# Layer 1 of a float32 decoder trunk: the first two SwiGLU pairs by seven products, and the sums of x on another engine

## The chip, the cores and the metric

One Trainium2 chip; the kernel runs on one of its cores. The core has a matrix engine (TensorE: PE for its matmuls, PEld for its weight loads, which overlap them), VectorE (DVE), ScalarE (ACT), GpSimd (POOL) and SyncE (SP, which issues most of the transfers from memory). Each of them takes its instructions in the order in which the program holds them, and waits at an instruction until the semaphores that it names have reached their values. The metric is the time of one execution on the device in microseconds (us), and the kernel before and the changed one are compared by it.

## What is computed

Two decoder layers over 512 tokens of 1024 channels, in float32. Layer 0 is a Conformer convolution block and a SwiGLU feed-forward; layer 1 is a sliding-window attention and a second SwiGLU feed-forward; a final RMSNorm ends it. The change lies in the feed-forward of layer 1, whose reference is this:

```python
def rmsnorm(x, g):
    xf = x.astype(jnp.float32)
    xf = xf * lax.rsqrt(jnp.mean(xf * xf, axis=-1, keepdims=True) + EPS)
    return (xf * g.astype(jnp.float32)).astype(x.dtype)

def swiglu_ffn(x, w_up, w_down):
    gate, up = jnp.split(x @ w_up, 2, axis=-1)
    return (jax.nn.silu(gate) * up) @ w_down
...
        h = h + swiglu_ffn(rmsnorm(h, norm_ffn[l]), ffn_w_up[l], ffn_w_down[l])
```

The hidden width is 2816, so `w_up` is 1024 x 5632 and `w_down` 2816 x 1024.

## The kernel before

**Float32 by three matmuls.** A float32 operand is held as two reduced-precision parts, hi and lo. `mm3` (its three matmuls are lines 380, 381 and 382) adds hi x hi, hi x lo and lo x hi. Weights come in chunks of 128 x 1024 floats (512 KB): SP loads a chunk into one of six `raw` tiles (line 261), ACT copies it to `whi` (line 294), and DVE subtracts to get `wlo` (line 297). Loads run up to nine chunks ahead of their use, the two splits three chunks ahead; `advance` does both. `PLAN` lists the chunks in the order in which TensorE takes them.

**Pairs.** The 22 slices of 128 hidden columns are worked off as 11 pairs. A plain pair (`plain_pair`) takes four chunks, `up` of half 0 and 1 of the channels for gate and up: 96 matmuls of 512 tokens. A pair by seven products (`SevenPair`, `seven_pair`) is a Winograd form of Strassen's scheme: the weight block and x are cut into 2 x 2 blocks (for x: `B11`, `B12`, `B21`, `B22`, channels by tokens), and seven products of sums of blocks take the place of eight. Each product is one chunk and 24 matmuls of 256 tokens, 168 for the pair. The products are named by their weight blocks: A11, A12, A22 are plain blocks, S1 to S4 are sums of blocks; their partners are B11, B21, T4, and T1, T2, T3 and B22 (`SEVEN`). So A11, A12 and S4 need no sum of x, and S1, S2, S3 and A22 do. `take` runs one product and moves its result out of PSUM into the four quarters of the pair's tile `up`; S2, S3, S4 and so on add into shared accumulation chains in PSUM (`CHAINS`): x for A11, S2, S3 and A22, z for S1 and S4, y for A12.

**Sums of weights.** S1 to S4 of every pair are made in memory by DMA while the kernel runs: SP copies one block (line 275), and a DMA issued by POOL adds the other onto it (line 289). `prepare` is the list of these, `share` says how many of them go with one chunk.

**Sums of x.** `Rows.sums` has ACT scale the eight slices of h into float32 tiles (line 753), then makes T1, T2, T3 and T4 one after the other (line 759, on POOL), each followed by its split into hi (ACT, lines 541 and 544) and lo (DVE, lines 542 and 545).

**The start of layer 1's feed-forward.** The output projection of the attention is added to h by DVE (line 1547); for each of the eight slices of h, ACT makes the hi part of the scaled x (line 536) and the square of h (line 487), DVE makes the lo part (line 537) and adds the square to the running sum (line 491). `Rms.step1` then has TensorE sum that over the channels with four short matmuls (line 503); DVE adds the epsilon (line 505), POOL takes the power -1/2 (line 507), DVE puts it on a diagonal (line 510). `step2` spreads it with one matmul (line 529), and the gates use it (lines 793 and 849).

The loop over `STEPS1` is: pair 0 plain, with the sums of x made beside it; pair 1 by seven products, with `flip` after each product (four transposes of h on TensorE, line 1562, and a copy by ACT, line 1563); pair 2 by seven; then the lower product `low` of pairs 0 and 1 (line 902), and so on to pair 10.

**What sets the order.** The program is written once in Python; a scheduler then places each engine's instructions by priorities and its own guess of when each is ready. So the order of the rows on each engine is part of the program, and is shown below where the change moves it.

Of the kernel before, what the change touches and what calls it, by code (L numbers as in the profile page):

```python
# [18 lines left out]
P = 128  # L19
# [4 lines left out]
FT = FF // P  # L24
# [13 lines left out]
STEPS1 = [("up", 0), ("up", 1), ("up", 2), ("low", 0)]  # L38
# [19 lines left out]
SEVENS = tuple(range(1, FT // 2))  # L58

def by_seven(layer, pair):  # L60
    return pair in SEVENS if layer else pair >= HALVES0[1][0]


def ups(layer, pair):
    return [("up", layer, pair, half, which) for half in range(2) for which in range(2)]
# [26 lines left out]
def chunk_plan():  # L92
# [12 lines left out]
    for part in range(2):  # L105
        pw2()
        for pair in range(*HALVES0[0]):
            plan.extend(ups(0, pair))
        downs(*HALVES0[0])
        if part == 0:  # L110
            plan.extend(("up0", pair, "A12") for pair in FIRST)
# [12 lines left out]
    for kind, pair in STEPS1:  # L124
        plan.extend(blocks_of(kind, pair) if kind == "low" or by_seven(1, pair) else ups(1, pair))
# [84 lines left out]
def hybrid_trunk(ctx: ExitStack, tc: tile.TileContext, xT, W, prm_in, wdw_in, sinks, relb, onehot, fin, lead, out):  # L210
# [524 lines left out]
    class Rows:  # L735
# [13 lines left out]
        def sums(self):  # L749
# [7 lines left out]
            for name, t, f, a, b in (("T1", t1, nc.gpsimd.tensor_sub, b11, b12), ("T2", b11, nc.gpsimd.tensor_add, b22, t1),  # L757
                                     ("T3", b12, nc.gpsimd.tensor_sub, b22, b12), ("T4", b21, nc.gpsimd.tensor_sub, b11, b21)):
                pool_op(f(t, a, b))
# [3 lines left out]
                split([both[:, e] for e in range(2)], t, name == "T2")  # L763

    def new_gates(pool):
        return pool.tile([P, 2, 2, 2, 256], F32, tag="up", name=uid("up"), bufs=3)

    def plain_pair(pair, rows, pool):

        banks = accs(512)  # L770
        steps = None
        for half in range(2):
            for which in range(2):
                w = get("up", 1, pair, half, which)
                order = [(k, m) for k in range(4) for m in range(2)]
                if half == 1:
                    order = [(k, m) for m in range(2) for k in range(4)]
                for k, m in order:
                    mm3(banks[which * 2 + m], [a[:, k, m * P:(m + 1) * P] for a in w], rows.x[half * 4 + k],
                        half == 0 and k == 0, half == 1 and k == 3)  # L780
                if half == 0 and which == 0:
                    rows.rms.step1()
                    continue

                if pair == 0:
                    steps = steps or rows.sums()
                    for _ in range(1 + half):
                        next(steps, None)
        rs_bc = rows.rms.step2().rearrange("p (s q) -> p s q", s=2)
        c = new_gates(pool)  # L790
        for m in range(2):
            t = temp()
            nc.vector.tensor_mul(t.rearrange("p (s q) -> p s q", s=2), banks[m].rearrange("p (s q) -> p s q", s=2), rs_bc)
            nc.scalar.activation(t, t, AF.Silu)
            nc.vector.tensor_mul(c[:, m, :, 0, :], banks[2 + m].rearrange("p (s q) -> p s q", s=2),
                                 t.rearrange("p (s q) -> p s q", s=2))
        return c
# [14 lines left out]
    class SevenPair:  # L812

        def __init__(self, kind, pair, rows, c, c11=None):
            self.kind, self.pair, self.rows, self.c, self.early = kind, pair, rows, c, c11
            self.chains = {}

        def take(self, a):
            c11, c12, c21, c22 = (self.c[:, m, s] for m in range(2) for s in range(2))
            chain = CHAINS[a][0]  # L820
# [10 lines left out]
            elif a == "S1":  # L831
                nc.scalar.mul(c22, r, -1.0)
            elif a == "S2":
# [517 lines left out]
    if True:  # L1351
# [10 lines left out]
        share[0] = 1  # L1362
# [204 lines left out]
    for kind, pair in STEPS1:  # L1567
# [6 lines left out]
        if by_seven(1, pair):  # L1574
# [3 lines left out]
        if pair == SEVENS[0]:  # L1578
            flip()
# [118 lines left out]
```

## Time and profile before

| | |
|---|---|
| runs | 1043.85 us median of 3 (1043.27 to 1044.0) |
| the profiled execution | 1043.27 us, of which the span from the first to the last instruction is 1041.5 us |
| mean granted TensorE clock | 0.997 |
| attention, to the end of the output projection | about 560 to 697 us of the span |
| pair 0 of layer 1 (plain) | about 697 to 720 us |
| pairs 1 and 2, with the first lower product | about 720 to 787 us |
| then every two pairs with a lower product | 59.7 us |

Times in the profile are microseconds from the start of the span. A row of the timeline gives start, duration, engine, line, operation, output<-input, partitions, shape and type, the number of instructions merged into the row, and in brackets how long the engine was idle before and what ended it. A matmul's recorded duration overlaps that of the next; the distance from start to start is what one costs in a row of them.

### The profile page before, as it was taken

To read this page: it belongs to the slowest core of one execution; us is meant where nothing else is said; L and a number is where in the kernel's file an instruction comes from. 1 tells how busy PE (TensorE), PEld (TensorE's weight loads), DVE (VectorE), ACT (ScalarE), POOL (GpSimd) and SP (SyncE) were. 2 spreads that over 40 slices of the span, in tenths; PEclk is the share of its full clock that TensorE was granted. 3 is DMA by queue.
4 is the path that set the end of the run, shared out by engine and by line. 5 is a ranking of instruction groups with operands and counts; after the bars stand their busy time and mean duration, and the time that the engine had idled before them with its cause. 6 is when DMAs were issued, how large, how long until landed. Compare 5 with 4: busy or idle time off the path is not lost.

```text
span 1041.5 us, 17709 instructions
## 1 busy us (share of the span) xinstructions
PE 1031.5 (99%) x6580; PEld 932.6 (90%) x6580; DVE 776.5 (75%) x1202; ACT 613.0 (59%) x1062; POOL 473.2 (45%) x569
## 2 busy tenths in 40 slices
PE   9999999999999999999999999999999999999996
PEld 8888889999988999998888877788989999898995
DVE  3999989978789777673536566678686877868777
ACT  3887798847776556552333565466655556554654
POOL 3999999930535233221214255405442334434134
PEclk9999999999999999999999999999999999999998
DMA  9999747999999988999969766955879988877742
GB/s 356 340 315 207 205 126 204 272 256 275 249 239 262 304 220 284 256 301 244 286 209 254 210 183 183 228 154 152 252 230 312 287 264 264 245 233 222 224 150 81
DMA packets 67282, 248.33 MB, mean 238 GB/s; under 512 B 7579, under 2 KB 13884, under 8 KB 66364
## 3 DMA queue, kind: packets, MB, share of 16 engines
q1 hardware_dynamic: 54236, 200.75, 55.9%
q0 software_dynamic: 12672, 46.14, 24.8%
q8 instruction: 51, 0.84, 0.3%
q10 hardware_dynamic: 288, 0.31, 0.1%
q14 instruction: 35, 0.29, 0.1%
HBM read 241.93 MB, written 97.52 MB: 326 GB/s over the span
## 4 chain that ended last, share of the span: by engine, by line
PE 98%; DMA 0%; DVE 0%; issue 0%; POOLq 0%; SPq 0%; POOL 0%; ACT 0%
PE bank L380 20%; PE bank L382 20%; PE bank L381 20%; PE bank L960 10%; PE bank L902 9%; PE bank L412 4%; PE bank L378 4%; PE bank L413 2%; PE bank L1441 1%; PE bank L1483 1%; PE bank L1470 1%; PE bank L1058 1%; PE bank L1607 1%; PE bank L948 1%; DMA both<-in_lead_dram 0%; PE bank L1562 0%
## 5 line engine op out<-in xcount | busy, mean ns | idle before, releaser
L297 DVE TENSOR_TENSOR wlo<-raw,whi 128x1024 fp32r<-128x1024 f32 x246 | 329.7, 1348 | 136.8 <-ACT whi L294 136.5
L294 ACT CAST whi<-raw 128x1024 fp32r<-128x1024 f32 x246 | 257.1, 1049 | 276.6 <-PE bank L381 194.1
L380 PE MATMUL bank<-quad,whi 128*128 128x256 f32 (+1 forms) x976 | 307.4, 317 | 0.0
L381 PE MATMUL bank<-quad,whi 128*128 128x256 f32 (+1 forms) x976 | 306.6, 315 | 0.0
L382 PE MATMUL bank<-quad,wlo 128*128 128x256 f32 (+1 forms) x976 | 305.7, 315 | 0.0
L380 PEld LDWEIGHTS bank<-quad,whi 128*128 128x128 f32 x976 | 185.5, 191 | 12.8 <-issue 1.6
L381 PEld LDWEIGHTS bank<-quad,whi 128*128 128x128 f32 x976 | 186.0, 191 | 11.9 <-issue 0.5
L382 PEld LDWEIGHTS bank<-quad,wlo 128*128 128x128 f32 x976 | 185.6, 191 | 11.8 <-issue 0.4
L853 POOL TENSOR_TENSOR up<-up 128x512 f32<-128x512 f32 x34 | 62.9, 1851 | 283.6 <-ACT up L850 283.6
L1002 POOL TENSOR_TENSOR pr<-pr,pr 128x256 f32<-128x256 f32 x208 | 155.4, 788 | 2.6 <-ACT pr L1001 2.5
L380 PE MATMUL bank<-rows,whi 128*128 128x256 f32 x488 | 138.0, 283 | 0.0
L381 PE MATMUL bank<-rows,whi 128*128 128x256 f32 x488 | 137.8, 282 | 0.0
L382 PE MATMUL bank<-rows,wlo 128*128 128x256 f32 x488 | 137.8, 282 | 0.0
L1009 DVE SCALAR_TENSOR_TENSOR bank<-apad,wdw,bank 128x256 f32<-128x256 f32 x248 | 112.4, 485 | 3.4
L1001 ACT ACTIVATE pr<-apad,wdw 128x256 f32<-128x256 f32 x208 | 98.3, 502 | 14.9 <-POOL pr L1002 13.1
L960 PE MATMUL bank<-quad,w 128*128 128x256 f32 x448 | 98.7, 380 | 0.0
L960 PEld LDWEIGHTS bank<-quad,w 128*128 128x128 f32 x448 | 84.9, 190 | 11.8 <-DVE bank L1009 0.2
L380 PEld LDWEIGHTS bank<-rows,whi 128*128 128x128 f32 x488 | 93.1, 191 | 0.3
L381 PEld LDWEIGHTS bank<-rows,whi 128*128 128x128 f32 x488 | 93.1, 191 | 0.3
L382 PEld LDWEIGHTS bank<-rows,wlo 128*128 128x128 f32 x488 | 93.0, 191 | 0.0
L491 POOL TENSOR_TENSOR tmp<-tmp,tmp 128x256 f32<-128x256 f32 (+1 forms) x28 | 26.8, 957 | 101.4 <-ACT tmp L487 96.2
L412 PE MATMUL bank<-quad,whi 128*128 128x512 f32 x168 | 59.7, 398 | 0.0
(230 smaller groups left out, 1635.9 us busy)
## 6 DMA issues: line engine op xcount, KB each, us to landing
raw<-in_W_dram SPq DMA_DIRECT2D x170, 512.0 KB, 5.7
raw<-sum SPq DMA_DIRECT2D x88, 512.0 KB, 5.4
sum<-in_W_dram SPq DMA_DIRECT2D x52, 512.0 KB, 6.2
sum<-in_W_dram POOLq DMA_DIRECT2D x44, 512.0 KB, 9.6
sum<-sum POOLq DMA_DIRECT2D x44, 512.0 KB, 8.5
sum<-in_W_dram SPq DMA_DIRECT2D x4, 3584.0 KB, 30.4
w<-in_W_dram SPq DMA_DIRECT2D x14, 512.0 KB, 8.6
sum<-in_W_dram SPq DMA_DIRECT2D x4, 1024.0 KB, 30.3
```

Of the source, the lines that this page charges most:

```text
L294: on_act = nc.scalar.copy(hi, src).ins
L297: latest[:] = [on_act, lo_engine[0].tensor_sub(lo, src, f32(hi)).ins]
L380: nc.tensor.matmul(out, w[0], x[0], start=start, stop=False, **kw)
L381: nc.tensor.matmul(out, w[0], x[1], start=False, stop=False, **kw)
L382: nc.tensor.matmul(out, w[1], x[0], start=False, stop=stop, **kw)
L412: nc.tensor.matmul(first[2], first[0], first[1], start=start, stop=False)
L853: pool_op(nc.gpsimd.tensor_mul(gate, gate, c[:, m, :, 1, :]))
L902: nc.tensor.matmul(out, x, w[:, ws], start=first and e == 0 and i == 0, stop=e == 1 and i == 2, skip_group_check=True)
L960: mm = nc.tensor.matmul(self.pb[:, w * W2:(w + 1) * W2], w1_of(ct, w, k), x[k] if x else xg[k][:, tok], start=k == 0, stop=k == KT - 1)
L1001: on_act = nc.scalar.mul(pr, a[:, j:j + W2], tap(j))
L1002: on_pool = pool_op(nc.gpsimd.tensor_add(pr, acc, pr))
L1009: on_dve = nc.vector.scalar_tensor_tensor(yt if i == nd - 1 else c, src, tap(i), c if i else self.shift, op0=ALU.mult, op1=ALU.add)
```

## The change

Pairs 0 and 1 are both done by seven products, as one step `("two", 0)`, in the order of the list `TWO`: A11 of both pairs, A12 of both, S4 of both (the six that need no sum of x), then S1, S2, S3, A22 of pair 0, and the same of pair 1. Since S4 now comes ahead of S1, S4 gets an accumulation chain of its own, "w" (`apart`), and its result is added on DVE to what S1 and S2 give. `step1` is called after the first product, and the eight flips after products 7 to 14. The sums of x, T1 to T4, are made by DVE in place of POOL, one step of them with most products and two with products 3 to 6. `share` is 1.2 in place of 1 from the key and value projection to the end of attention, since four more sums of weights are due. `plain_pair` goes.

```diff
-STEPS1 = [("up", 0), ("up", 1), ("up", 2), ("low", 0)]
+STEPS1 = [("two", 0), ("up", 2), ("low", 0)]
+TWO = [(p, a) for a in ("A11", "A12", "S4") for p in range(2)] + [(p, a) for p in range(2) for a in ("S1", "S2", "S3", "A22")]
...
-        plan.extend(blocks_of(kind, pair) if kind == "low" or by_seven(1, pair) else ups(1, pair))
+        plan.extend([("up", *step) for step in TWO] if kind == "two" else blocks_of(kind, pair))
...
-            for name, t, f, a, b in (("T1", t1, nc.gpsimd.tensor_sub, b11, b12), ("T2", b11, nc.gpsimd.tensor_add, b22, t1),
-                                     ("T3", b12, nc.gpsimd.tensor_sub, b22, b12), ("T4", b21, nc.gpsimd.tensor_sub, b11, b21)):
-                pool_op(f(t, a, b))
+            yield
+            for name, t, f, a, b in (("T1", t1, nc.vector.tensor_sub, b11, b12), ("T2", b11, nc.vector.tensor_add, b22, t1),
+                                     ("T3", b12, nc.vector.tensor_sub, b22, b12), ("T4", b21, nc.vector.tensor_sub, b11, b21)):
+                with tc.issue_after(latest[1]):
+                    f(t, a, b)
                 yield
...
                 split([both[:, e] for e in range(2)], t, name == "T2")
+                yield
...
-    def plain_pair(pair, rows, pool):
...
-        def __init__(self, kind, pair, rows, c, c11=None):
+        def __init__(self, kind, pair, rows, c, c11=None, apart=False):
...
-            chain = CHAINS[a][0]
+            chain = "w" if self.apart and a == "S4" else CHAINS[a][0]
...
             elif a == "S1":
                 nc.scalar.mul(c22, r, -1.0)
+                if self.apart:
+                    nc.vector.tensor_add(c12, r, c12)
+            elif self.apart and a in ("S2", "S4"):
+                (nc.scalar.copy if a == "S4" else lambda o, i: nc.vector.tensor_add(o, i, c12))(c12, r)
...
-        share[0] = 1
+        share[0] = 1.2
...
-        if by_seven(1, pair):
-            c = seven_pair("up", pair, nxt, new_gates(pool7), flip if pair == SEVENS[0] else None)
-        else:
-            c = plain_pair(pair, nxt, pool7)
-        if pair == SEVENS[0]:
-            flip()
+        if kind == "two":
+            two = [SevenPair("up", p, nxt, new_gates(pool7), apart=True) for p in range(2)]
+            steps = nxt.sums()
+            for n, (p, a) in enumerate(TWO):
+                two[p].take(a)
+                if n == 0:
+                    nxt.rms.step1()
+                for _ in range((1, 2)[n in (2, 3, 4, 5)]):
+                    next(steps, None)
+                if n >= 6:
+                    flip()
+                if a == "A22":
+                    forms[p] = forms_of(two[p].gates(), pool7, p % 2)
+            continue
+        c = seven_pair("up", pair, nxt, new_gates(pool7))
```

In the changed program most lines stand a little higher: `mm3` is lines 376 to 378, `step1`'s matmuls are line 499, the split of weights lines 290 (ACT) and 293 (DVE), the sums of x line 757.

TensorE, where `step1` stands. Before, in pair 0: `quad_7167` and `quad_7168` are hi and lo of the second half of x's channels, `quad_7165` and `quad_7166` those of the first, and `tmp_7353` is the finished sum of squares.

```order
L381 MATMUL bank_7356<-quad_7168,whi_7362 128x512
L382 MATMUL bank_7356<-quad_7167,wlo_7363 128x512
L381 MATMUL bank_7357<-quad_7168,whi_7362 128x512
L503 MATMUL bank_7390<-ones_c,tmp_7353 128x1 x4
L380 MATMUL bank_7358<-quad_7165,whi_7304 128x512
L381 MATMUL bank_7358<-quad_7166,whi_7304 128x512
```

In the changed program, at the end of the first product (A11 of pair 0, into `bank_7370`) and the start of the second (A11 of pair 1, into `bank_7424`); `tmp_7365` is the finished sum of squares:

```order
L377 MATMUL bank_7370<-quad_7175,whi_7283 128x256
L378 MATMUL bank_7370<-quad_7174,wlo_7284 128x256
L499 MATMUL bank_7402<-ones_c,tmp_7365 128x1 x4
L376 MATMUL bank_7424<-quad_7174,whi_7316 128x256
L377 MATMUL bank_7424<-quad_7175,whi_7316 128x256
L378 MATMUL bank_7424<-quad_7174,wlo_7317 128x256
```

Before, 47 matmuls of 512 tokens of pair 0 stand ahead of the four matmuls of `step1`; now 24 matmuls of 256 tokens do. Up to the first matmul of pair 0 TensorE's order is the same in both programs, and so is that of DVE and ACT up to the last addition of squares.

VectorE from that last addition (`tmp_7353` before) on. Before, `wlo` are weight splits, `rows` the lo parts of sums of x, `ms` and the product with `ident` belong to the norm:

```order
L491 TENSOR_TENSOR tmp_7353<-tmp_7347,tmp_7353 128x512
L297 TENSOR_TENSOR wlo_7449<-raw_7176,whi_7448 128x1024
L545 TENSOR_TENSOR rows_7476<-t_7441,rows_7476 128x1024
L505 TENSOR_SCALAR ms_7395<-bank_7390 128x4
L542 TENSOR_SCALAR rows_7480<-quad_7431,rows_7480 128x1024
L545 TENSOR_TENSOR rows_7514<-quad_7431,rows_7514 128x1024
L297 TENSOR_TENSOR wlo_7487<-raw_7209,whi_7486 128x1024
L510 TENSOR_TENSOR tmp_7399<-ident,rs_7397 128x512
```

In the changed program (`wlo_7464` is the split for S4 of pair 0, `wlo_7500` for S4 of pair 1, `wlo_7536` for S1 of pair 0; line 757 makes T1, T2, T3):

```order
L487 TENSOR_TENSOR tmp_7365<-tmp_7359,tmp_7365 128x512
L757 TENSOR_TENSOR t_7423<-quad_7413 128x1024
L501 TENSOR_SCALAR ms_7407<-bank_7402 128x4
L506 TENSOR_TENSOR tmp_7411<-ident,rs_7409 128x512
L1543 TENSOR_SCALAR nrs<-rs_7409 128x4
L293 TENSOR_TENSOR wlo_7464<-raw_7185,whi_7463 128x1024
L757 TENSOR_TENSOR quad_7413<-quad_7414,t_7423 128x4x256
L541 TENSOR_TENSOR rows_7492<-t_7423,rows_7492 128x1024
L538 TENSOR_SCALAR rows_7528<-quad_7413,rows_7528 128x1024
L293 TENSOR_TENSOR wlo_7500<-raw_7221,whi_7499 128x1024
L757 TENSOR_TENSOR quad_7413<-quad_7414,quad_7413 128x4x256
L808 TENSOR_TENSOR up_7368<-bank_7457,up_7368 128x512
```

The norm's instructions now stand ahead of the split for S4 of pair 0, and the four sums of x and their lo parts share DVE's queue with the splits.

More of the change, by code (lines that the diff above doesn't have):

```diff
@@ L57, with ups @@
 SEVEN = ("A11 B11", "S1 T1", "S2 T2", "A12 B21", "S3 T3", "S4 B22", "A22 T4")
[L58 to L65, printed above, removed]
+def ups(pair):
+    return [("up", 0, pair, half, which) for half in range(2) for which in range(2)]
 SUMS = {"S1": ("A21", "A22"), "S2": ("A11", "S1"), "S3": ("A21", "A11"), "S4": ("A12", "S2")}
@@ L107, in chunk_plan @@
         for pair in range(*HALVES0[0]):
-            plan.extend(ups(0, pair))
+            plan.extend(ups(pair))
         downs(*HALVES0[0])
```

29 lines of the change are left out of this document (1 added, 28 removed).

## The prediction

> **What bounds the kernel now.** I read the page first: who is busy, and the chain of work that ended last.
>
> ```profile
> PE 1031.5 (99%) x6580; PEld 932.6 (90%) x6580; DVE 776.5 (75%) x1202; ACT 613.0 (59%) x1062; POOL 473.2 (45%) x569
> PE 98%; DMA 0%; DVE 0%; issue 0%; POOLq 0%; SPq 0%; POOL 0%; ACT 0%
> ```
>
> TensorE is the chain. The view of its waits, next, names two, both in the first 8 us:
>
> ```profile
> PE bank L465 <- POOL ones_m L462: 1.1, 1, 1.1
> PE bank L948 <- DVE quad L922: 0.7, 2, 0.4
> ```
>
> So time is won only by fewer or shorter matmuls, and lost by any new wait of TensorE. The question is what both are at the start of layer 1's feed-forward. TensorE's timeline there, and three rows of the chain further on:
>
> ```profile
> 696.75 0.39 PE L380 MATMUL bank<-quad,whi 128*128 128x512 f32 x1
> ...
> 707.18 0.39 PE L381 MATMUL bank<-quad,whi 128*128 128x512 f32 x1
> 707.41 0.95 PE L503 MATMUL bank<-ones_c,tmp 128*128 128x1 f32 x8
> 708.21 0.49 PE L380 MATMUL bank<-quad,whi 128*128 128x512 f32 x1
> ```
>
> ```profile
> 821.03 5.52 PE bank L902 x24
> 829.42 11.09 PE bank L902 x48
> 880.73 5.52 PE bank L902 x24
> ```
>
> Pair 0 begins at 696.75; 47 matmuls stand ahead of step1 at 707.41, so one of 512 tokens costs 10.66 / 47 = 0.227 us. From 821.03 to 880.73 lie two pairs by seven (336 matmuls of 256) and one lower product (84 of line 902, at 11.09 / 48 = 0.231, 19.4 us): one of 256 tokens costs (59.70 - 19.4) / 336 = 0.120 us.
>
> **TensorE's work.** Pair 0 loses 96 x 0.227 = 21.8 us and gets 168 x 0.120 = 20.1 us: **1.6 us less**. The eight flips, the four matmuls of step1 and the spread of the norm move but stay as many. This is all that the change can give, since TensorE waits for nothing that it removes.
>
> **The new wait.** step1 now stands behind 24 matmuls of 256. TensorE takes them in order, so it comes to step1 at 696.75 + 24 x 0.120 = 699.63. What step1 reads is the last sum of squares, and DVE makes it here:
>
> ```profile
> 697.57 0.68 DVE L1547 TENSOR_TENSOR h<-bank,h 128x512 f32<-128x512 f32 x1
> 698.17 0.68 DVE L491 TENSOR_TENSOR tmp<-tmp,tmp 128x512 f32<-128x512 f32 x1
> 698.77 1.22 DVE L297 TENSOR_TENSOR wlo<-raw,whi 128x1024 fp32r<-128x1024 f32 x1
> 699.90 0.74 DVE L537 SCALAR_TENSOR_TENSOR quad<-h,prm,quad 128x512 fp32r<-128x512 f32 x1
> 700.57 0.68 DVE L491 TENSOR_TENSOR tmp<-tmp,tmp 128x512 f32<-128x512 f32 x1
> 701.17 0.74 DVE L537 SCALAR_TENSOR_TENSOR quad<-h,prm,quad 128x512 fp32r<-128x512 f32 x1
> 701.83 0.68 DVE L491 TENSOR_TENSOR tmp<-tmp,tmp 128x512 f32<-128x512 f32 x1
> ```
>
> Without a pause from 697.57 on, it ends at 701.83 + 0.68 = 702.51, and up to there the three engines' orders are unchanged, so it ends there in the changed kernel too. Before, TensorE came to step1 4.9 us after it; now it comes 2.88 us ahead. How fast a waiting TensorE starts shows at the very start of the trace:
>
> ```profile
> 3.96 0.35 DVE L922 TENSOR_SCALAR quad<-both,prm 128x256 f32<-128x256 f32 x1 [3.09 <-DMA prm<-in_prm_dram]
> 4.36 0.29 PEld L948 LDWEIGHTS bank<-quad,both 128*128 128x128 f32 x1 [0.68 <-DVE quad L922]
> ...
> 706.95 0.19 PEld L381 LDWEIGHTS bank<-quad,whi 128*128 128x128 f32 x1
> ```
>
> DVE ended at 4.31, the weight load began at 4.36: 0.05 us. The load itself takes 0.19 us and can't go ahead here, since its operand is what is waited for. So step1 begins at 702.51 + 0.05 + 0.19 = 702.75 in place of 699.63: **3.1 us lost**. Bounds: 2.9 (neither of the two small terms) to 3.4 (the first matmul behind it as slow as behind step1 above, 0.33 from 708.21 on against 0.23, and a slower semaphore). Behind step1 in TensorE's queue stand A11 of pair 1 and all the rest, and A11 of pair 1 was ready: its splits come well ahead.
>
> **What is late next.** step1 takes 0.8 us (707.41 to 708.21), so product 2 begins at 703.55, and each product takes 24 x 0.120 = 2.88. I follow DVE's new order from 702.5. It holds 128x1024 operations, for which these rows of DVE, POOL and ACT give prices:
>
> ```profile
> 705.96 8.07 DVE L297 TENSOR_TENSOR wlo<-raw,whi 128x1024 fp32r<-128x1024 f32 x1 [3.44 <-ACT whi L294]
> 716.29 1.22 DVE L545 TENSOR_TENSOR rows<-quad,rows 128x1024 fp32r<-128x1024 f32 x1
> 724.96 1.65 DVE L297 TENSOR_TENSOR wlo<-raw,whi 128x1024 fp32r<-128x1024 f32 x1 [0.25 <-ACT whi L294]
> 707.93 5.01 POOL L759 TENSOR_TENSOR quad<-quad,quad 128x1024 f32<-128x1024 f32 x2
> 715.32 1.96 POOL L507 TENSOR_TENSOR rs<-ms,mhalf 128x4 f32<-128x4 f32 x1 [2.38 <-DVE ms L505]
> 699.96 5.02 ACT L753 ACTIVATE quad<-h,prm 128x512 f32<-128x512 f32 x8
> 704.88 1.04 ACT L294 CAST whi<-raw 128x1024 fp32r<-128x1024 f32 x1
> ```
>
> A sum of x on DVE isn't in the trace. Below stands 1.2 us, a subtraction of the same shape beside an idle POOL; above 1.65, beside a working one. (The 8.07 us is a DVE operation that stood until POOL's sums of x were done; with those gone from POOL that goes too, but TensorE didn't wait for it.) I take 1.2, since POOL has no large operation there now. T1 from 702.5 to 703.7; then the norm, which waits for step1 and for POOL's 1.96 us, so its DVE part ends at about 706.6; the split for S4 of pair 0 ends at 707.8. Product 5 (S4 of pair 0) begins at 703.55 + 3 x 2.88 = 712.2: 4.4 us to spare. Up to the split for S1 of pair 0 DVE has six more of 1.2 and one of 0.7, to about 715.7; product 7 begins at 718.0: 2.3 us to spare. Its ACT part is no later: the scaling of x ends at 705.0, and ACT then needs about 1.05 us for each of three splits, the first two sums' hi parts and two copies, to 712.6. Behind product 7 each further product brings a 1.2 us split and a 0.7 us addition to DVE against 2.88 us and the flips on TensorE, so the distance grows. The sums thus cost nothing under this cover of 2.3 us; it is there because step1 waits. Without the wait of step1 it would be about gone.
>
> **Transfers.** Three more chunks are loaded, four more copies and four more additions issued, half of them far ahead of use. The extra additions fall in the attention:
>
> ```profile
> L289 POOL DMA_DIRECT2D sum<-in_W_dram x7 | 5.9, 979 | 0.0
> L1460 POOL TENSOR_SCALAR sc<-sc,sm 128x256 f32<-128x256 f32 (+1 forms) x64 | 31.4, 505 | 44.0 <-DVE sm L1458 43.7
> ```
>
> ```profile
> 697.00:707.00 10.00, 10.00 (x46) 8.29 (x45) 6.56 (x9) 9.87 (x15) 4.34 (x3) 1.00 0.36 117
> 821.00:880.70 59.70, 59.70 (x422) 56.11 (x421) 45.24 (x50) 32.53 (x42) 21.51 (x19) 1.00 0.88 275
> ```
>
> An addition takes POOL 0.98 us to issue; four take 4 us of the 44 in which POOL, by its groups from 575 to 690 us, waits for DVE there. Behind them are the softmax's scalings, which TensorE's transposes read; their cost is 0 under that cover, and up to 1 us each if one meets a scaling. The opening of pair 0 uses the DMA engines 0.36 of the time against 0.88 in the steady part (the last two rows, of the windows; the share is the last number but one), which feeds pairs by seven at the same pace. I take 0.
>
> **Sum.** -1.6 + 3.1 + 0 = **+1.5 us**. Against the profiled execution, 1043.27 us (a span of 1041.5 and 1.8 around it), that is 1044.8; the median before is 0.58 above that execution, so the forecast for the median is **1045.4 us**, +0.15%. A change within 0.2%, 2.1 us, can hardly be told from none here.
>
> **Rivals.**
>
> *The clock drops in the wait.* TensorE has no long pause before, but it has one at the end. Its last matmul in the timeline, the windows there (the granted clock is the last number but two), and a row of the timeline and one of the chain on the price:
>
> ```profile
> 1033.05 0.28 PE L1607 MATMUL bank<-whi,hid 128*128 128x256 f32 x1
> ```
>
> ```profile
> 1032.80:1036.20 3.40, 0.53 (x5) 0.32 (x3) 3.18 (x9) 2.55 (x8) 1.65 (x3) 1.00 0.62 231
> 1036.20:1036.30 0.10, 0.00 (x0) 0.00 (x0) 0.10 (x1) 0.00 (x0) 0.10 (x1) 0.70 0.00 0
> ```
>
> ```profile
> 1.05 2.93 PE L465 MATMUL bank<-ones_m 128*128 128x128 f32 x12 [1.05 <-POOL ones_m L462]
> ...
> 593.13 1.46 PE bank L1470 x12
> ```
>
> The last matmul ended at 1033.33, and the clock fell between 1036.20 and 1036.30, 2.9 us later; the new pause is 2.7 to 2.9 us. At half clock a matmul costs twice: 12 took 2.93 us at the cold start against 1.46 later. That start lasted at least these 2.93 us; an episode of 3 to 6 us would lose 1.5 to 3 us more. Time 1045.4 + 1.5 to 3, say **1047.6**. [...] Chance 0.18.
>
> *DVE becomes the bound.* If its fifteen 128x1024 operations between the sum of squares and S1 of pair 1 take 1.65 us in place of 1.2, that is 6.7 us against a cover of 2.3: 4.4 us more, 1049.8; with half of that inflation 1 us, 1046.4. Against it: POOL has only its short power and issues there. Say **1047.5**, chance 0.16.
>
> *No wait.* If the squares are done when TensorE comes, all of the 1.6 us is won: **1042.2**. It needs DVE 2.9 us earlier, and DVE has no pause to give. Chance 0.10.
>
> *The change doesn't do what it says* (the pairs run, but a transfer of a weight sum is late): for S4 of pair 0, the first sum used, a landing late by one median of POOL's additions, 9.1 us, less the 4.4 us spare, gives 1050. Chance 0.04.
>
> **How the numbers follow.** The forecast has 0.50, its own range 1044.6 to 1046.4 from the bounds of the wait and the 0.7 us between the runs before; the cases above 0.18, 0.16, 0.10 and 0.04, and 0.02 for the unforeseen. Slower by over 0.2% is above 1045.94: a quarter of the forecast's range (0.13), nearly all of clock, DVE and late transfer (0.35): 0.48. Faster is below 1041.76: the case without a wait ends just inside, so 0.06 for it with luck. The rest, 0.46, is within. The range from 1042.1 to 1047.9 holds the forecast, the case without a wait and the lower halves of the others.
>
> **What would show it.** Right: an idle time of TensorE of about 3 us ahead of step1's line, released by DVE's addition of squares, and no other over 0.3 us up to the first lower product; DVE's 8 us row gone; the same granted clock. Wrong: no pause there; a granted clock under 1 in a window from 703 to 710; pauses ahead of S1 to A22 of pair 0 that end with a `rows` or `wlo` of DVE; a scaling in the attention that ends a pause of TensorE.

## The result, and the profile after

| | before | changed |
|---|---|---|
| median of six runs each | 1043.92 us (1043.27 to 1044.3) | 1048.55 us (1047.03 to 1049.71) |
| ratio of the changed kernel's times to those before, 95% interval | | 1.0046, 1.0033 to 1.0059 |
| the profiled execution (span) | 1043.27 us (1041.5) | 1047.03 us (1045.3) |
| mean granted clock, run by run | 0.997 (profiled) | 0.997, 0.996, 0.996, 0.995, 0.994, 0.996 |

The changed kernel is slower: by 4.6 us between the medians, by 0.46% in the ratio. The forecast was 1045.4 and its range ended at 1047.9, so the time lies outside it, on the slow side.

The page first: who is busy, and the shares of the chain that ended last.

```profile
PE 1032.0 (99%) x6652; PEld 936.1 (90%) x6652; DVE 781.4 (75%) x1212; ACT 618.3 (59%) x1069; POOL 468.0 (45%) x571
PE 97%; DVE 1%; issue 1%; DMA 0%; ACT 0%; POOLq 0%; POOL 0%; DVEq 0%
```

At this level the two kernels look alike: PE has lost one point of the chain, and DVE and "issue" have one each. The view of TensorE's waits says what is new:

```profile
PE bank L499 <- DVE tmp L487: 2.8, 1, 2.8
PE bank L378 <- DVE wlo L293: 0.9, 1, 0.9
```

(Total us, times, the longest.) Neither was there before. The first is the wait that was forecast, at step1. The second was not forecast. TensorE's timeline shows both, and a third thing that no view of waits can show:

```profile
696.18 0.28 PE L376 MATMUL bank<-quad,whi 128*128 128x256 f32 x1
...
698.93 0.28 PE L378 MATMUL bank<-quad,wlo 128*128 128x256 f32 x1
702.00 1.05 PE L499 MATMUL bank<-ones_c,tmp 128*128 128x1 f32 x8 [2.79 <-DVE tmp L487]
...
704.47 0.42 PE L376 MATMUL bank<-quad,whi 128*128 128x256 f32 x1
...
707.85 0.28 PE L377 MATMUL bank<-quad,whi 128*128 128x256 f32 x1
...
784.37 0.39 PE L378 MATMUL bank<-quad,wlo 128*128 128x256 f32 x1 [0.94 <-DVE wlo L293]
...
824.57 0.63 PE L874 MATMUL bank<-whi,fhi 128*128 128x512 f32 x2
```

From 698.93 to 702.00 are 3.07 us where a matmul takes 0.12: **2.95 us of wait**. (The rows count two records for each plain float32 matmul: x8 are the four of step1.) Behind it the matmuls run at 0.12 us each for a while, and then, from 704.47 to 707.85, 16 of them take 0.21. The windows between the borders of that stretch (PE's busy time and count come second, the granted clock is the last number but two):

```profile
697.54:700.95 3.41, 1.67 (x14) 1.47 (x13) 3.41 (x6) 3.41 (x7) 0.00 (x0) 1.00 0.21 19
700.95:704.36 3.41, 2.36 (x20) 2.36 (x21) 2.29 (x4) 3.41 (x7) 0.93 (x1) 1.00 0.70 288
704.36:707.77 3.41, 3.41 (x18) 3.41 (x18) 3.17 (x5) 2.41 (x4) 1.85 (x3) 0.50 0.52 84
707.77:711.18 3.41, 3.41 (x30) 3.41 (x30) 3.36 (x3) 3.35 (x4) 0.00 (x0) 1.00 1.06 222
```

The granted clock is 0.50 for 3.41 us and 1.00 on both sides. It falls 2.4 us after TensorE has taken up work again, which is why the pause and the slow matmuls don't touch in the timeline. Cost: 3.38 us for 16 matmuls that take 1.92 at full clock, **1.46 us**. TensorE is "busy" all the while, so neither the busy shares nor the waits show it.

DVE's new work at the start of the feed-forward runs as the sum had it: T1 takes 1.23 us, the splits about it the same, and there is no row of 8 us.

```profile
702.05 1.23 DVE L757 TENSOR_TENSOR t<-quad 128x1024 f32<-128x1024 f32 x1
```

The second new wait lies 80 us later, in the first lower product. The rows of DVE and POOL that lead to it in the changed kernel, and below them those of the same place before (lines 297 and 909 there):

```profile
780.00 4.32 DVE L293 TENSOR_TENSOR wlo<-raw,whi 128x1024 fp32r<-128x1024 f32 x1
...
780.41 2.81 POOL L881 TENSOR_TENSOR h<-h,tmp 128x512 f32<-128x512 f32 x2
```

```profile
777.62 1.68 DVE L297 TENSOR_TENSOR wlo<-raw,whi 128x1024 fp32r<-128x1024 f32 x1
...
779.88 1.21 DVE L297 TENSOR_TENSOR wlo<-raw,whi 128x1024 fp32r<-128x1024 f32 x1
...
776.92 1.30 POOL L909 TENSOR_TENSOR h<-h,tmp 128x512 f32<-128x512 f32 x1
...
780.41 1.83 POOL L909 TENSOR_TENSOR h<-h,tmp 128x512 f32<-128x512 f32 x1
```

A split that takes 1.2 us by itself takes 4.32 in the changed kernel, until about 1.1 us after POOL's two additions to h have ended (780.41 + 2.81 = 783.22). Before, the two additions stand apart, with another operation of POOL and the issue of a transfer between them. The first meets a split for 0.6 us, and that split takes 1.68; the second begins 0.53 us into a split that takes its 1.21 all the same, and there it is the addition that takes 1.83 in place of 1.30. In the changed kernel TensorE waits 0.94 us for the split of 4.32, with the restart **1.1 us** (783.15 to 784.37 for one matmul).

**The account.** The stretch from pair 0's first matmul to the first of the lower product of pairs 2 and 3 holds everything that the change moves. Before, it ends here:

```profile
820.86 1.09 PE L902 MATMUL bank<-whi,fhi 128*128 128x512 f32 x4
```

It takes 820.86 - 696.75 = 124.11 us before and 824.57 - 696.18 = 128.39 after: +4.28. The wait (2.95), the half clock (1.46) and the held split (1.1) make 5.51; the rest, -1.23, is what the seven products gain less what is lost in small places. Behind this stretch both kernels take the same time to their last matmul, 212.19 us (1033.05 before, 1036.76 after). The median of the runs lies 1.5 us above the profiled execution, and the runs with the lower mean clocks are the longer ones; the experiments show why.

### The profile page after: what moved, and what is told of

The parts are those of the page before. It is cut to its first block, busy times and chain, and to the rows that moved or that the text cites. A ratio compares the mean times of both kernels' runs of the same rounds, so it can differ in the third digit from the quotient of the medians.

```text
span 1045.3 us, 17886 instructions
## 1 busy us (share of the span) xinstructions
PE 1032.0 (99%) x6652; PEld 936.1 (90%) x6652; DVE 781.4 (75%) x1212; ACT 618.3 (59%) x1069; POOL 468.0 (45%) x571
## 4 chain that ended last, share of the span: by engine, by line
PE 97%; DVE 1%; issue 1%; DMA 0%; ACT 0%; POOLq 0%; POOL 0%; DVEq 0%
PE bank L376 20%; PE bank L378 20%; PE bank L377 20%; PE bank L932 10%; PE bank L874 9%; PE bank L408 4%; PE bank L374 4%; PE bank L409 2%; PE bank L1413 1%; PE bank L1455 1%; PE bank L1442 1%; PE bank L1030 1%; PE bank L1588 1%; PE bank L920 1%; DVE wlo L293 1%
## 5 line engine op out<-in xcount | busy, mean ns | idle before, releaser
L290 ACT CAST whi<-raw 128x1024 fp32r<-128x1024 f32 x249 | 260.2, 1050 | 268.0 <-PE bank L377 178.7
L376 PE MATMUL bank<-quad,whi 128*128 128x256 f32 (+1 forms) x968 | 302.0, 314 | 0.0
L378 PE MATMUL bank<-quad,wlo 128*128 128x256 f32 (+1 forms) x968 | 301.0, 312 | 0.9 <-DVE wlo L293 0.9
L377 PE MATMUL bank<-quad,whi 128*128 128x256 f32 (+1 forms) x968 | 301.6, 312 | 0.0
L825 POOL TENSOR_TENSOR up<-up 128x512 f32<-128x512 f32 x36 | 65.9, 1831 | 307.7 <-ACT up L822 307.7
L376 PE MATMUL bank<-rows,whi 128*128 128x256 f32 x520 | 147.4, 284 | 0.0
L377 PE MATMUL bank<-rows,whi 128*128 128x256 f32 x520 | 146.9, 282 | 0.0
L378 PE MATMUL bank<-rows,wlo 128*128 128x256 f32 x520 | 146.8, 282 | 0.0
L376 PEld LDWEIGHTS bank<-rows,whi 128*128 128x128 f32 x520 | 99.2, 191 | 0.5 <-ACT h L1535 0.2
L377 PEld LDWEIGHTS bank<-rows,whi 128*128 128x128 f32 x520 | 99.2, 191 | 0.5 <-issue 0.2
L378 PEld LDWEIGHTS bank<-rows,wlo 128*128 128x128 f32 x520 | 99.2, 191 | 0.0
```

What stands on the lines that cost most here:

```text
L290: on_act = nc.scalar.copy(hi, src).ins
L376: nc.tensor.matmul(out, w[0], x[0], start=start, stop=False, **kw)
L377: nc.tensor.matmul(out, w[0], x[1], start=False, stop=False, **kw)
L378: nc.tensor.matmul(out, w[1], x[0], start=False, stop=stop, **kw)
L825: pool_op(nc.gpsimd.tensor_mul(gate, gate, c[:, m, :, 1, :]))
```

## The experiments

The theory after these profiles: the loss is a wait of 2.95 us at step1, the clock that this wait brings down, and a split that POOL holds up at 780; the pairs by seven gain what was expected. The rivals: the pairs, the sums on DVE or the transfers are dearer than thought, and the wait only shows it; or the fall of the clock is chance. The kernel before was run beside each group of runs, and its median lay between 1043.64 and 1044.85 us, so times are compared by the ratio to it. In the profiled executions pair 0 begins anywhere from 696.18 to 698.76 us, also in kernels that are the same up to there, so whole profiled times can't be compared to a microsecond. Times of stretches are read as in the account: from the first matmul of pair 0 to the first of the lower product of pairs 2 and 3, against 124.11 before.

**step1 after the third product.**

```diff
-                if n == 0:
+                if n == 2:
                     nxt.rms.step1()
```

> The changed kernel with step1 called after the third product instead of the first. TensorE then comes to it at about 705.4, some 2.9 us after DVE's last addition of squares (702.5). Theory (the loss is the wait of 2.8 to 3.0 us ahead of step1, and the clock that falls because of it): no idle time ahead of step1, granted clock 1.00 from 697 to 712, and 1042.5 us (1047.03 of the profiled run, less 3.0 of the wait and 1.5 of the 16 slow matmuls), with runs that lie as close together as those of the kernel before. Rival (the two pairs by seven, the sums of x on DVE or the extra transfers cost the time, and the wait only shows it): 1047 us or more, the wait reappearing ahead of a later product.

Measured: 1045.12 us, ratio 1.0002 (0.9993 to 1.0011), mean clocks 0.997 or 0.998 in all eleven runs. TensorE's timeline:

```profile
698.70 0.28 PE L376 MATMUL bank<-quad,whi 128*128 128x256 f32 x1
...
707.21 0.28 PE L378 MATMUL bank<-quad,wlo 128*128 128x256 f32 x1
707.33 0.50 PE L499 MATMUL bank<-ones_c,tmp 128*128 128x1 f32 x4
...
823.08 0.63 PE L874 MATMUL bank<-whi,fhi 128*128 128x512 f32 x2
```

step1 follows the matmul before it at 0.12 us: no wait, and the mean granted clock of this execution is 0.998. The stretch is 124.38, 4.01 us shorter than in the changed kernel. This rules the rival out for these 4 us: pairs, sums and transfers are all still there. By the ratios the gain on the changed kernel is 0.44%, 4.6 us, where 4.5 were expected; the absolute 1042.5 was too low, since it started from the shortest of the changed kernel's six runs and the kernel before took 0.9 us more beside this run. It is not faster than the kernel before, since the held split (1.13 us, at 782) is left, and a pause of 0.18 us at 735, 0.45 with the slower matmuls around it, is new.

**The pause filled with work.** Ten matmuls on constants ahead of step1, in its bank; their results are not used. `issue_after` only fixes the order of the instructions; the lines that hand it the matmuls before and behind are not shown (...).

```diff
...
+            for i in range(warm):
+                with tc.issue_after(last):
+                    last = nc.tensor.matmul(st[:, 3 * P:], ones_m, ones_m, start=True, stop=True).ins
             for i in range(n):
...
-                    nxt.rms.step1()
+                    hold[0] = nxt.rms.step1(10, two[p].mm)
...
```

> The changed kernel with ten more matmuls of 128x128 on constants (about 2.4 us at full clock, results unused) put between the last matmul of the first product and step1, so that TensorE waits as before for the squares but is idle for only some 0.4 us. Theory (clock): the four matmuls of step1 begin at the same 702.0 as before, the granted clock stays 1.00 there, the 16 matmuls take 0.12 us each, and the time is 1045.5 us, 1.5 under the profiled run of the changed kernel and 3 under its median, with the spread of the runs gone. Rival (the wait alone costs, the clock's episode is chance or comes from something else): the clock falls all the same, 1047 to 1049 us.

Measured: 1047.82 us, ratio 1.0026 (1.0015 to 1.0036), mean clocks 0.997 to 0.999.

```profile
698.76 0.28 PE L376 MATMUL bank<-quad,whi 128*128 128x256 f32 x1
...
701.63 2.39 PE L500 MATMUL bank<-ones_m 128*128 128x128 f32 x20
704.58 1.05 PE L502 MATMUL bank<-ones_c,tmp 128*128 128x1 f32 x8 [0.55 <-DVE tmp L487]
...
825.48 0.40 PE L881 MATMUL bank<-whi,fhi 128*128 128x512 f32 x1
```

```profile
701.60:705.40 3.80, 3.25 (x30) 3.06 (x28) 3.70 (x6) 3.80 (x7) 0.00 (x0) 1.00 0.78 276
705.40:712.20 6.80, 6.80 (x59) 6.80 (x59) 5.55 (x8) 6.80 (x10) 2.78 (x3) 1.00 0.55 97
```

step1 starts 3.07 us after the last real matmul (701.51), as in the changed kernel, so the wait is untouched; but the clock stays at 1.00, and the stretch is 126.72, 1.67 us shorter than in the changed kernel's first profile: the 1.46 of the half clock, and some 0.2 of the held split, for which TensorE waits 0.7 us here. Work that computes nothing makes this kernel faster, although the intervals of the two ratios still touch. The spread of the runs shrinks too, from 2.7 to 1.1 us. So the fall of the clock is an effect of the idle time, and the waiting itself costs what the sum gave it. The absolute expectation, 1045.5, was low: the kernel before took 1044.85 beside this run, 0.9 more than beside the changed one, and the expected 3 us under the changed kernel's median came out as 0.20% of the time, 2.1 us, by the ratios.

**The kernel before, with the same wait.** step1 after 12 matmuls of plain pair 0 in place of 47; the rest only fixes the order of the matmuls around it (the helper lines are not shown).

```diff
...
-                for k, m in order:
-                    mm3(banks[which * 2 + m], [a[:, k, m * P:(m + 1) * P] for a in w], rows.x[half * 4 + k],
-                        half == 0 and k == 0, half == 1 and k == 3)
+                for n, (k, m) in enumerate(order):
+                    if pair == half == which == 0 and n == 4:
+                        early = rows.rms.step1(early)
+                    with tc.issue_after(early) if early is not None else nullcontext():
+                        early = mm3(banks[which * 2 + m], [a[:, k, m * P:(m + 1) * P] for a in w], rows.x[half * 4 + k],
+                                    half == 0 and k == 0, half == 1 and k == 3)
...
```

> The kernel before, plain pair 0 and sums of x on POOL, with nothing changed but step1's place: after 12 matmuls of 512 tokens in place of 47, so that TensorE comes to it at about 699.5, the same 2.9 us too early. Theory (wait and clock make the loss, whatever products stand around them): an idle time of about 2.9 us, a fall of the clock to half two to three us after it, and 1048.3 us or more (1043.9 + 2.9 + 1.5 for each period at half clock). Rival (wait alone): 1046.8 us with the clock at 1. Rival (the loss belongs to the seven products): under 1045 us.

Measured: 1050.73 us, ratio 1.0053 (1.0040 to 1.0065), mean clocks 0.995 to 0.997.

```profile
697.81 0.39 PE L380 MATMUL bank<-quad,whi 128*128 128x512 f32 x1
...
703.63 1.46 PE L504 MATMUL bank<-ones_c,tmp 128*128 128x1 f32 x8 [2.94 <-DVE tmp L491]
...
705.52 0.63 PE L381 MATMUL bank<-quad,whi 128*128 128x512 f32 x1
...
828.33 0.63 PE L906 MATMUL bank<-whi,fhi 128*128 128x512 f32 x2
```

```profile
700.70:704.11 3.41, 0.48 (x5) 0.48 (x5) 2.88 (x5) 3.41 (x7) 0.40 (x1) 1.00 0.54 145
704.11:707.52 3.41, 3.41 (x12) 2.93 (x12) 0.50 (x2) 2.96 (x5) 3.41 (x3) 0.50 0.40 162
707.52:710.94 3.42, 3.42 (x9) 2.65 (x9) 3.42 (x1) 0.91 (x1) 3.42 (x3) 0.50 0.88 153
```

The stretch is 130.52, +6.41 against the kernel before: 3.1 for the wait (700.31 to 703.63, less one matmul), and twice 3.41 us at half clock, in which 14 matmuls of 512 take 0.427 us in place of 0.227 (2.9 with the ends) and step1 itself 0.4 more. One instruction that comes too early makes the old kernel, with pair 0 plain as ever, at least as slow as the changed one (its two profiled stretches are 128.39 and 129.83). Here the half clock costs as much as the wait.

**The changed kernel again,** beside other runs of the kernel before.

> The changed kernel itself, beside the kernel before, on the chip of these runs. If the wait (about 2.9 us), at least one period at half clock (1.5 us for 3.4 us of it, 2.7 to 2.9 for 6 us) and the held split (1.1 us) stand against a gain of 1.2 to 1.6 us, it is 4.3 to 5.7 us above the kernel before: 1048.9 to 1050.6 where that has 1044.85. If the result so far belonged to one chip alone, under 1047.

Measured: 1048.83 us beside 1043.64, ratio 1.0045 (1.0033 to 1.0058), mean clocks 0.995 to 0.997. So the result repeats. In its profile the pause is the same 2.79 us, but the half clock lasts two periods of 3.41 us, and the stretch takes 129.83, 1.44 more than in the first profile:

```profile
698.95:702.36 3.41, 0.93 (x8) 0.72 (x7) 3.41 (x5) 3.41 (x7) 0.00 (x0) 1.00 0.39 89
702.36:705.77 3.41, 3.11 (x14) 3.11 (x15) 1.64 (x3) 3.41 (x6) 0.96 (x1) 0.50 0.52 219
705.77:709.19 3.42, 3.42 (x18) 3.42 (x17) 3.31 (x5) 1.83 (x4) 1.82 (x3) 0.50 0.54 86
```

That is the 1.5 us by which the runs of one kernel differ: one period at half clock or two, 1.5 or about 3 us. The first profile was of the cheap kind; the times and mean clocks of the other runs suggest that most of them were not, but those were not profiled.

**Shorter pauses:** four constant matmuls, and seven.

> The kernel with constant matmuls ahead of step1, with four of them in place of ten: about 1 us of work at the start of the pause, so that TensorE is idle for some 2.0 us instead of 0.55 or 2.8. The wait is as long as ever. If the clock falls only when an idle time of about 2.8 us is seen, it stays at 1.00 and the time is that with ten, 1047.8 us, with mean clocks of 0.997 to 0.999. If a shorter idle time is enough, the clock falls in this one too, with 1.4 to 2.9 us more: 1049.2 to 1050.7 and mean clocks of 0.994 to 0.996.

> Seven constant matmuls ahead of step1, about 1.7 us of work, so that an idle time of about 1.2 us is left; the wait is as long as ever. Idle times so far: 0.55 us left the clock alone, 1.89 us brought it to half for 3.4 us. If what counts is an idle time near 2 us, the clock stays at 1.00 and the time is 4.2 us or less above the kernel before (wait 2.9, held split 1.1, gain 1.3, constant matmuls nothing: +2.7). If 1.2 us is enough, 1.5 to 3 us more.

Measured: with four 1048.33 us, ratio 1.0043 (1.0029 to 1.0056); with seven 1047.57 us, ratio 1.0040 (1.0025 to 1.0056). step1's row and the window behind it, of the first and of the second:

```profile
703.21 1.05 PE L502 MATMUL bank<-ones_c,tmp 128*128 128x1 f32 x8 [1.89 <-DVE tmp L487]
```

```profile
705.53:708.94 3.41, 3.41 (x19) 3.41 (x18) 3.14 (x5) 2.44 (x4) 1.89 (x3) 0.50 0.53 88
```

```profile
703.27 1.05 PE L502 MATMUL bank<-ones_c,tmp 128*128 128x1 f32 x8 [1.22 <-DVE tmp L487]
```

```profile
705.40:712.00 6.60, 6.60 (x57) 6.60 (x57) 6.08 (x7) 5.54 (x8) 2.08 (x3) 1.00 0.74 139
```

An idle time of 1.89 us was enough for a full period at half clock in the profiled run, so the first of the two cases expected, a fall only near 2.8 us, is out. It may not bring a fall each time: one of the four runs, 1046.86 us at a mean clock of 0.998, looks like one without, but was not profiled. With 1.22 us the profiled run kept its clock. Its four runs fall in two pairs, 1046.79 and 1047.04 us at a mean clock of 0.998, 1048.10 and 1048.85 at 0.996, which is what one would see if the clock fell in two of them; those two were not profiled, so the case of 1.22 us stays undecided. Ten matmuls (0.55 us idle) are on the safe side: no run under 0.997.

**A12 of the first lower product on DVE.**

```diff
-                if a == "A12":
+                if a == "A12" and pair:
                     m = temp()
                     nc.scalar.mul(m, out, scale)
```

> The changed kernel, but in the first lower product (pair 0) the block A12 is scaled and added to h in one operation by DVE, as the other blocks are, in place of ACT's scaling and POOL's addition. This takes away POOL's two additions of 1.4 us beside which a split of weights on DVE took 4.32 us at 780. Theory: the idle time of 0.94 us at 784.37 goes, 1047.4 us or 1.1 us under the changed kernel. Rival (DVE's own two operations delay the splits as much): no difference, 1048.5 us.

Measured: 1049.21 us, ratio 1.0042 (1.0029 to 1.0054). One of DVE's splits at that place, in the timeline (the next, from 782.05 on, takes as long):

```profile
780.26 1.22 DVE L293 TENSOR_TENSOR wlo<-raw,whi 128x1024 fp32r<-128x1024 f32 x1
```

The long split is gone, and so is TensorE's idle time there. The trace shows what that is worth: from 697.70 to 826.43 the stretch is 128.73 us, 1.10 less than in the changed kernel's second profile (129.83), which has the same pause of 2.79 us and two periods at half clock as well. The median doesn't show it: the runs have mean clocks of 0.994, in one case 0.996, and the ratio can't be told from the changed kernel's 1.0045. While the clock falls for one period or two, 1.1 us can't be read from medians of this size. For that it needs a kernel without the pause, which is the next one.

**Both: step1 after the third product, and A12 on DVE.** The edits are the two above.

> step1 after the third product and A12 of the first lower product on DVE, both together. Theory: neither the wait with its slow clock nor the stall of 1.1 us at about 782 is left; what remains is the gain of the two pairs, 1.2 to 1.6 us less the 0.45 us at 735: 1044.0 us where the kernel before has 1044.85, and the first version that is faster than it. Rival (DVE's two additional operations hold a later split as long as POOL's did): 1045.1 us, no difference to step1 after the third product alone.

> The version with step1 after the third product and A12 of the first lower product on DVE, once more beside the kernel before: 0.8 us less than it, if the gain was not chance; the reference for the version that alternates the pairs.

Measured: 1042.79 us beside 1043.64, ratio 0.9990 (0.9982 to 0.9999); and again 1042.98 beside 1043.87, ratio 0.9992 (0.9983 to 1.0001). Both times 0.9 us faster than the kernel before, though the second interval reaches 1.0001. The waits of TensorE behind the opening of the kernel are one, and the stretch (second run) is the shortest of all:

```profile
PE bank L376 <- DVE up L810: 0.2, 1, 0.2
```

```profile
697.55 0.28 PE L376 MATMUL bank<-quad,whi 128*128 128x256 f32 x1
...
820.71 0.63 PE L874 MATMUL bank<-whi,fhi 128*128 128x512 f32 x2
```

123.16 us, 0.95 less than before. With the 0.45 us that the remaining pause costs, the pairs by seven gain 1.4 us. Against step1 after the third product alone, the ratio falls from 1.0002 to 0.9990 and 0.9992: that is the 1.1 us of the held split.

**The pairs in turns.** S1, S2, S3 and A22 alternate between the two pairs, which is meant to take away the last pause.

```diff
-TWO = [(p, a) for a in ("A11", "A12", "S4") for p in range(2)] + [(p, a) for p in range(2) for a in ("S1", "S2", "S3", "A22")]
+TWO = [(p, a) for a in ("A11", "A12", "S4", "S1", "S2", "S3", "A22") for p in range(2)]
```

> As the version with step1 after the third product and A12 of the first lower product on DVE, but S1, S2, S3 and A22 taken in turns of the two pairs instead of all of pair 0 first, so that between two products that add into one PSUM chain another product stands. Theory: the pause of 0.18 us (0.45 us with the slower matmuls around it) at 734, where the last product of pair 1 waits for DVE to read the chain, goes; 0.4 us under that version and 1.2 to 1.3 us under the kernel before. Rival (both pairs' gates now come together, and DVE and ACT hold the splits of pair 2): a wait for wlo between 736 and 750, no gain or 1 us more.

Measured: 1043.9 us, ratio 0.9998 (0.9989 to 1.0008), so 0.6 to 0.8 us are lost against the version before it, where 0.4 were to be gained. The pause at 734 is gone, and a longer one has come at pair 2:

```profile
758.75 0.39 PE L376 MATMUL bank<-rows,whi 128*128 128x256 f32 x1 [1.10 <-ACT up L806]
```

```profile
755.41 0.42 ACT L537 ACTIVATE fhi<-up 128x256 fp32r<-128x256 f32 x1 [2.31 <-POOL up L848]
...
758.12 0.58 ACT L806 COPY up<-bank 128x512 f32<-128x512 f32 x1
```

Not a split but ACT's copy of a chain of pair 2 ends it (line 806). ACT comes to it late, since ahead of it in its queue stand the hi parts of the second pair's sums of gated blocks (lines 537 and 540), for which it waits 2.31 us until POOL has added them up behind those of the first. Half of the theory held, and the rival was right on the sum and wrong on the engine and the place.

**The sums of x back on POOL,** with step1 after the third product.

```diff
-            for name, t, f, a, b in (("T1", t1, nc.vector.tensor_sub, b11, b12), ("T2", b11, nc.vector.tensor_add, b22, t1),
-                                     ("T3", b12, nc.vector.tensor_sub, b22, b12), ("T4", b21, nc.vector.tensor_sub, b11, b21)):
+            for name, t, f, a, b in (("T1", t1, nc.gpsimd.tensor_sub, b11, b12), ("T2", b11, nc.gpsimd.tensor_add, b22, t1),
+                                     ("T3", b12, nc.gpsimd.tensor_sub, b22, b12), ("T4", b21, nc.gpsimd.tensor_sub, b11, b21)):
...
-                    f(t, a, b)
+                    pool_op(f(t, a, b))
```

> step1 after the third product, and the four sums of x made by POOL as in the kernel before, in place of DVE. POOL's sums take 2.5 us each (5.0 for two in the trace of before), and DVE's split beside them took 8 us there. Theory (moving the sums to DVE is needed, since DVE's splits for S4 have no 8 us to spare): one or two waits of TensorE for a wlo or rows of DVE between 708 and 725, together 2 to 6 us, 1047 to 1051 us. Rival (the sums' engine makes no difference, since the six first products cover either): 1045.1 us as with the sums on DVE.

Measured: 1047.28 us, ratio 1.0036 (1.0024 to 1.0048), mean clocks 0.996 to 0.998. The matmul that waits, the split that it waits for, and POOL beside it:

```profile
712.20 0.38 PE L378 MATMUL bank<-quad,wlo 128*128 128x256 f32 x1 [2.16 <-DVE wlo L293]
```

```profile
706.95 5.20 DVE L293 TENSOR_TENSOR wlo<-raw,whi 128x1024 fp32r<-128x1024 f32 x1
...
706.08 2.65 POOL L757 TENSOR_TENSOR quad<-quad,t 128x1024 f32<-128x1024 f32 x1
708.45 2.61 POOL L757 TENSOR_TENSOR quad<-quad,quad 128x1024 f32<-128x1024 f32 x1
```

The split for S4 of pair 0 takes 5.20 us, until POOL's second sum is through. TensorE waits 2.16 us for it, and again the clock goes to half for 3.41 us behind it (712.82 to 716.23). So in this order of products the move of the sums to DVE is worth some 3.5 us (1.0036 against 1.0002), more than the pairs by seven gain.

## Why the prediction was wrong, point by point

- **What bounds the kernel:** right. TensorE is 97 to 98% of the chain in both, and every loss found is a pause of TensorE or its clock.
- **TensorE's work, -1.6 us:** nearly right. With all waits of the change out of the way it is -1.4 (the version with step1 after the third product and A12 on DVE). Where the other 0.2 went was not traced.
- **The new wait, +3.1 us** (bounds 2.9 to 3.4)**:** right in place, releaser and size: 2.95 us, ended by DVE's last addition of squares. With step1 two products later it is gone.
- **What is late next, 0:** right as far as it was followed, to S1 of pair 0 and on to the end of the two pairs: no pause there, the sums of x at 1.23 us where 1.2 was taken, and DVE's row of 8 us gone. It failed behind that. "Behind product 7 ... the distance grows" was argued from DVE's queue alone; in the first lower product the changed order sets POOL's two additions to h one behind the other, and a split of DVE stands until both are done: 1.1 us.
- **Transfers, 0:** right. From a matmul at the end of the attention's projections (561.29 before, 560.74 after) to pair 0 it is 135.46 us before and 135.44 after.
- **The clock:** this is the main step that failed: the sum had it at nothing. "The clock drops in the wait" stood among the rivals with 0.18. Its price was right: 1.5 to 3 us were given, one period of 3.41 us at half clock cost 1.46 and two about 3. The 3 to 6 us that a fall would last were the author's estimate; it lasted 3.41 us in three profiles and 6.8 in three others. The factor of two was read off the first matmuls of the trace, where the profile of the kernel before has a granted clock of 1.00 (1.05 to 3.98 us), so for the half clock it was an estimate too; at a granted clock of 0.50 the factor was 1.8 to 1.9 (0.21 for 0.12, 0.427 for 0.227). The fall 2.9 us after the last matmul at the end of the trace doesn't say that 2.9 us are needed: in the first profile it came 2.4 us after the pause had ended, with TensorE busy for 1.67 and 2.36 us of the two windows of 3.41 us before it, and pauses of 2.79, 2.16 and 1.89 us were all followed by a fall.
- **The sum.** -1.4 + 2.95 + 1.46 + 1.1 = +4.1 us for the profiled execution, where 3.8 were measured on the time and 4.28 on the stretch; with two periods at half clock +5.6. The forecast held the first two terms, left out the third as a rival that it thought unlikely, and did not have the fourth.
- **"DVE becomes the bound", "No wait" and the late transfer of a weight sum:** none of them came. Of the two new waits of TensorE one is that of step1, and the other is for a split held by POOL; none ends with a transfer.
- **What would show it:** the list named a granted clock under 1 between 703 and 710 as the sign of being wrong, and that is where it was.

## What to carry to other kernels

A pause of the matrix engine is not priced by its length alone: here those of 1.89 to 2.94 us brought one or two periods of 3.41 us at half clock in their profiles, and the longest without, of the eight read below, was 1.22 us. Look for them in the granted clock by windows, after the pause, where every view of waits is silent. An instruction with one late operand in an in-order queue belongs behind work that is ready (here two products further, for 4 us), and if there is no such work, matmuls on constants in the pause can pay for themselves (here 2.1 us). When an order is changed, follow the engines whose operations took longer beside each other's (a split 4.32 us beside two additions of POOL, 1.22 by itself) through the next stage too, not just to the end of the edited one: the 1.1 us of the held split lay some 80 us behind step1, between two engines whose work there the edit never named.

## What the hardware showed that was not expected

*When the clock falls.* Eight profiles with a pause have been read by windows of 3.41 us, the shortest half clock seen, back from the fall:

| kernel | idle time | idle in the last 3.41 us before the fall | half clock |
|---|---|---|---|
| changed, first profile | 2.79 | 1.05 (and 1.74 in the 3.41 us ahead of these) | one period |
| four constant matmuls | 1.89 | 1.09 (and 0.80 in those ahead) | one period |
| sums of x on POOL | 2.16 | 2.16 | one period |
| changed, again | 2.79 | 2.48 | two periods |
| A12 on DVE | 2.79 | 2.79 | two periods |
| kernel before, early step1 | 2.94 | 2.93 | two periods |
| seven constant matmuls | 1.22 | | none |
| the pairs in turns | 1.10 | | none |

The last 3.41 us before the fall, of the third and of the fifth line of the table:

```profile
709.41:712.82 3.41, 1.25 (x11) 1.05 (x10) 3.41 (x3) 3.41 (x4) 3.41 (x3) 1.00 0.12 22
```

```profile
700.57:703.98 3.41, 0.62 (x6) 0.46 (x5) 3.31 (x6) 3.41 (x6) 0.00 (x0) 1.00 0.75 239
```

In these six falls the half clock lasted 3.41 us or twice that (6.8), and twice that where the 3.41 us ahead of the fall held 2.48 us or more of idle time. In the first profile the clock stayed at 1.00 behind a window with 1.74 us of idle time and fell behind the next, with 1.05; what decides on a fall was not shown.

*POOL and DVE.* In three places a split of DVE lasted until the run of POOL's operations had ended and then some 1.1 us more: 4.32 us beside two additions back to back, 5.20 beside two sums of x, 1.68 where one POOL operation was nearly over; 1.22 where nothing holds it. Not every meeting holds the split. With A12 on DVE, the splits of 780.26 and 782.05 took 1.22 each, and it was POOL's three operations on 128x256, recorded from 779.60 on, that took 4.26 us together, where one took 0.74 in the kernel before (at 776.22, with DVE idle); the split of 779.88 in the kernel before is of this kind too. Two of DVE's operations that read PSUM took 1.40 us there, from 781.01 on, under POOL's addition of 780.41 to 782.24, and two took 1.40 in the changed kernel, from 784.24 on, while POOL only issued transfers. The recorded starts don't tell which of the two is held: the split of 5.20 us began 0.87 us behind POOL's first sum and was held, and of the two that began ahead of POOL's addition, by 0.41 and by 0.53 us, the first was held and the second was not.
